# Ordering edges behind the two state copies of an RWKV-7 chain step

## The chip, the cores and the metric

One core of a Trainium2 chip runs the kernel. The metric is the device time of one launch in microseconds (us), lower is better. Before the change it is 1561.51 us, the median of three runs (1561.48 to 1563.06).

## What is computed

A decoder layer for one sequence of 1024 tokens and width 1024. One RMSNorm and one input projection feed two branches of 16 heads of 64 channels: RWKV-7 time mixing, which is a recurrence, and causal attention with three dilated windows. Each branch has a SiLU gate; the concatenated branches go through an output projection, a residual addition and a final RMSNorm. The change touches the recurrence alone:

```python
def step(state, inp):
    r_t, w_t, k_t, v_t, av_t, bv_t = inp
    sa = jnp.einsum('bhvk,bhk->bhv', state, av_t)
    state = (state * w_t[:, :, None, :] + sa[..., None] * bv_t[:, :, None, :]
             + v_t[..., None] * k_t[:, :, None, :])
    return state, jnp.einsum('bhvk,bhk->bhv', state, r_t)
```

## The kernel before

The program runs in three stages: the RWKV stage, with all projections of that branch woven in (the first 850 us), the attention stage with its own projections, and the output projection. Only the first is touched.

**Units and steps.** The 16 heads are taken as 8 pairs, and the 1024 tokens as two halves of 512, which gives 16 units. Inside a unit the recurrence is done in chunks of 64 tokens, 8 per unit, and each chunk in three steps of the `chain` (L636): `first` multiplies the state `Sd` into `z`, `second` multiplies `zd` with the inverted triangular matrix `U` into the other half of `z`, `third` multiplies `ud` into `T`. Each step is a TensorE (PE) matmul into PSUM followed by `spread` (L653), the **two copies** of the step: VectorE (DVE) copies one head's 64x64 block to SBUF (L656 or, with a scale, L659), ScalarE (ACT) the other's (L657, L660). The copies make `zd`, `ud` or the next `Sd`, which is the operand of the next step's matmul. So a unit is a serial chain of 24 steps: PE, then DVE and ACT, then PE again. Steps are counted here from 0, the first `z<-Sd` of a unit, to 23; copy n follows the matmul of step n, and step n+1 needs it.

**What is woven in.** `rwkv` (L297) has 24 slots (`NSLOT`) per unit, one for each chain step. Into each slot's list `ev[s]` go the chain step of unit p, and, at slots from the tables at the head of the file, the work on its neighbours: `finish` of unit p-1 (group norm and gate), `late` and `invert` of unit p+1 (transposes, and the inversion whose 15 column eliminations are two small DVE operations each, L570 into `TB` and L572 into `UB`, followed by a round trip through DRAM, L579 and L583, and four block steps of small matmuls m1 to m4, L590 to L634), `prepare` and `products` of unit p+2 (decays, products, masks, L394 to L554). After the list of a slot, `advance(n)` (L206) emits n = 4 matmuls (`pq`, L187) of the projections that later units and the attention stage need, with the loads, casts and subtractions of their weights (L176 to L179) and the work on their results (L221, L224, L257, L259).

**What sets the order.** Nothing of this is issued in the order written. The Tile framework schedules when the program is built: the priority of an instruction is its place in the program, and an engine is given the first ready instruction by priority. Where the head of the queue is not ready in its model, work from later slots is taken ahead. The order so found is fixed, and on the chip each engine runs its own list strictly in order, with semaphores between engines. The chain's steps come first in their slots:

```python
for s in range(NSLOT):
    for f in ev[s]:
        f()
    self.advance(n)
```

Of the kernel before, what the change touches and what calls it, by code (L numbers as in the profile page):

```python
# [12 lines left out]
AF = mybir.ActivationFunctionType  # L13
ALU = mybir.AluOpType
# [39 lines left out]
class Kern:  # L54
# [237 lines left out]
    def rwkv(self, pairs=range(NPAIR), apairs=range(NPAIR)):  # L292
        nc = self.nc
        with ExitStack() as ctx:
            P = lambda n, b=1, s=None: self.pool(n, b, s, ctx)
            self.ps_a = P("ps_a", 1, PSUM)
            self.ps_z = P("ps_z", 1, PSUM)  # L297
            self.ps_y = P("ps_y", 1, PSUM)
            self.ps_tr = P("ps_tr", 1, PSUM)
            self.mid = P("mid", 2)  # L300
            self.inv = P("inv", 1)
            self.pers = pers = P("pers")
            self.lng = P("lng", 3)
            self.dpool = P("dpool", 2, bass.MemoryType.DRAM)
            self.carry = pers.tile([128, 25], F32, name="carry")
            self.Us = [pers.tile([128, NC_ + 1, C], F32, name=f"U{i}") for i in range(2)]
            self.Vds = [pers.tile([128, NC_, 2, HD], F32, name=f"Vd{i}") for i in range(2)]
            self.Sds = [pers.tile([128, 2, HD], F32, name=f"Sd{i}") for i in range(2)]
            self.llo = [pers.tile([128, 128], F32R, name=f"llo{i}") for i in range(2)]
            self.zds, self.uds = ([pers.tile([128, 2, HD], F32, name=f"{nm}{i}") for i in range(2)] for nm in ("zd", "ud"))  # L310
            for u in self.Us + self.Vds + self.Sds + self.zds + self.uds:
                nc.gpsimd.memset(u, 0.0)
            for u in self.llo:
                nc.gpsimd.memset(u.bitcast(F32), 0.0)
            self.ARs = [pers.tile([128, NC_ * 192 + 2], F32, name=f"AR{i}") for i in range(3)]
            for a in self.ARs:
                nc.gpsimd.memset(a[:, NC_ * 192:], 0.0)
                a = self.c192(a)
                for e in range(2):
                    er = slice(e * 64, e * 64 + 64)  # L320
                    nc.gpsimd.tensor_copy(out=a[er, :, 0], in_=bc(self.ident[er, er].unsqueeze(1), (64, NC_, 64)))
            self.d0 = pers.tile([128, 2, C + 1], F32, name="d0")
            self.lw = pers.tile([128, NC_, C + 1], F32, name="lw")
            nc.gpsimd.memset(self.lw, 0.0)
            nc.gpsimd.memset(self.d0, 1.0)
            nc.gpsimd.memset(self.d0[:, :, C:C + 1], 0.0)
            bank = lambda p, tag: lambda: p.tile([128, 4, 128], F32, name="xq", tag=tag)
            ba = [bank(self.ps_a, "pa0"), bank(self.ps_a, "pa1")]
            tags = ("MV", "MV", "MV", "TU", "TU", "BK")
            for _ in self.prep_x(0, self.lng, tags, [bank(self.ps_proj, "proj")] * 2 + ba):  # L330
                pass
            units = [dict(h=h, pr=pr) for pr in pairs for h in range(2)]
            for i, d in enumerate(units):
                d["AR"], d["Vd"] = self.ARs[i % 3], self.Vds[i % 2]
            N = len(units)
            self.flow = self.stream(self.jobs(units, apairs))
            next(self.flow)
            self.taken = 1
            self.params(self.lng.tile([P_N, 128], F32, name="rows", tag="TU"),
                        self.ps_tr.tile([128, P_N], F32, name="prm_ps", tag="tr"))  # L340
            self.advance(6 * KT - 1)
            get = lambda n: units[n] if 0 <= n < N else None
            self.lora_w(units[0])
            for p in range(-2, N):
                dA, dI, dC, dF = get(p + 2), get(p + 1), get(p), get(p - 1)
                ev = [[] for _ in range(NSLOT)]
                put = lambda steps: [ev[s].append(f) for s, f in steps]
                if dC:
                    put(enumerate(self.chain(dC, get(p + 1) if dC["h"] == 0 else None)))
                if dF:  # L350
                    put(self.finish(dF))
                if dI:
                    put(self.late(dI))
                    put(self.invert(dI, self.Us[(p + 1) % 2]))
                if dA:
                    lag = WARM[p + 2] if p < 0 else 0
                    put([(n + lag, f) for n, f in self.prepare(dA) + self.products(dA)])
                if get(p + 3) and get(p + 3)["h"] == 0:
                    ev[12].append(lambda d=get(p + 3): self.lora_w(d))
                elif get(p + 3):  # L360
                    get(p + 3)["lw"] = get(p + 2)["lw"]
                if p == -2:
                    px = self.prep_x(1, self.lng, tags, ba)
                    for s in range(4):
                        ev[s].append(lambda: [next(px, None) for _ in range(2)])
                    ev[4].append(lambda: [None for _ in px])
                n = 5 if p < 0 else 2 if dA is not None and get(p + 3) is None else 4
                for s in range(NSLOT):
                    for f in ev[s]:
                        f()  # L370
                    self.advance(n)
            for _, f in self.finish(units[-1]):
                f()

# [261 lines left out]
    def chain(self, d, nxt):  # L636
# [3 lines left out]
        V, S, G = nc.vector, nc.scalar, nc.gpsimd  # L640
# [12 lines left out]
        def spread(out, q, scale):  # L653

            if scale is None:
                V.tensor_copy(out=out[er[0], 0], in_=q[0:64, 0:64])  # L656
                S.copy(out=out[er[1], 1], in_=q[0:64, 64:128])  # L657
            else:
                V.tensor_scalar(out=out[er[0], 0], in0=q[0:64, 0:64], scalar1=scale[0], scalar2=None, op0=ALU.mult)  # L659
                S.activation(out=out[er[1], 1], in_=q[0:64, 64:128], func=AF.Copy, scale=scale[1])  # L660

        def first(c):
            AR = d["AR"]
# [14 lines left out]
        def third(c):  # L678
            T = d["T", c // 4][:, c % 4]
            if c == 5:  # L680
                self.heads_out(d, 0)
            mm(T, f2(d["TU"][:, c])[:, 0:128], self.uds[c % 2], False, True)
            if c == NC_ - 1 and nxt is None:
                G.memset(self.Sds[0], 0.0)
                return
            dec, n = (nxt["dec"], 0) if c == NC_ - 1 else (d["dec"], c + 1)
            spread(self.Sds[(c + 1) % 2], T, [dec[:, e, n:n + 1] for e in range(2)])
            if n:
                values(n)
# [412 lines left out]
```

## Time and profile before

| | |
|---|---|
| median of three runs | 1561.51 us |
| the profiled execution's own time | 1562.53 us |
| its span, first to last instruction | 1560.8 us |
| PE busy | 1490.8 us, 96% |
| DVE busy | 1029.8 us, 66% |
| ACT busy | 891.8 us, 57% |
| GpSimd busy | 455.3 us, 29% |
| granted TensorE clock, mean | 0.997 |

The span leaves out 1.7 us around it. PE is busy nearly always, and what it waits is 70 us in all. A busy share over the whole span hides that the stages differ, so the profile is read stage by stage, and in the RWKV stage piece by piece within a unit, which repeats every 47.4 us. The instruction that waits on an engine is named with what released it; the releaser is inferred from semaphores.

### The profile page before, as it was taken

The numbers are of one execution on the slowest core, as the hardware profiler recorded it, in microseconds if no ns is written. First come the engines' busy times: TensorE is split into PE (matmuls) and PEld (weight loads), VectorE is DVE, ScalarE is ACT, GpSimd is POOL, SyncE is SP. The second block draws the span as 40 slices with busy tenths as digits, with TensorE's granted clock in tenths as the row PEclk, the third lists the DMA queues.
The fourth block names the chain that finished last, engine by engine and source line by source line (L and its number), as shares of the span: only waits on it lengthen the run. The fifth ranks groups of instructions, "written<-read, shape, count | busy, mean of one in ns | idle before, by whom it ended". The sixth has DMA issues, their size and how long they took to land.

```text
span 1560.8 us, 29095 instructions
## 1 busy us (share of the span) xinstructions
PE 1490.8 (96%) x10721; PEld 1211.8 (78%) x10721; DVE 1029.8 (66%) x2776; ACT 891.8 (57%) x2080; POOL 455.3 (29%) x563
## 2 busy tenths in 40 slices
PE   5999999999999999999999999999999999899997
PEld 4777777777777777777677788888888888787886
DVE  6867876777866768767644557666686676856144
ACT  6556666666666666665653556555565665645221
POOL 3122111121201212112111434333343344456442
PEclk9999999999999999999999999999999999999999
DMA  6221111111111111111111201111111111426452
GB/s 198 66 66 40 39 34 41 45 34 48 32 42 40 42 38 45 27 41 46 31 31 43 70 28 42 35 35 34 35 55 28 41 55 55 155 96 196 144 163 98
DMA packets 178829, 94.87 MB, mean 61 GB/s; under 512 B 58413, under 2 KB 164606, under 8 KB 178686
## 3 DMA queue, kind: packets, MB, share of 16 engines
q1 hardware_dynamic: 174942, 86.19, 19.4%
q10 hardware_dynamic: 3744, 6.82, 1.3%
q8 instruction: 84, 1.38, 0.4%
q14 instruction: 59, 0.48, 0.1%
HBM read 75.01 MB, written 17.83 MB: 59 GB/s over the span
## 4 chain that ended last, share of the span: by engine, by line
PE 67%; DVE 18%; ACT 10%; issue 3%; DMA 1%; POOL 1%; DVEq 0%; SPq 0%; POOLq 0%; ACTq 0%
PE pq L187 33%; PE oq L986 10%; PE T L645 4%; PE z L645 3%; PE o L932 3%; PE mp L859 2%; PE sp L892 2%; PE pa L529 2%; PE sp L912 1%; PE sp L911 1%; ACT zt L726 1%; DVE wl L179 1%; ACT MV L535 1%; PE x L621 1%; DVE I L424 1%
## 5 line engine op out<-in xcount | busy, mean ns | idle before, releaser
L187 PE MATMUL pq<-xh,wh 128*128 128x512 f32 x1040 | 428.9, 413 | 0.0
L187 PE MATMUL pq<-xl,wh 128*128 128x512 f32 x1040 | 416.4, 400 | 0.0
L187 PE MATMUL pq<-xh,wl 128*128 128x512 f32 x1040 | 294.8, 404 | 0.0
L187 PEld LDWEIGHTS pq<-xl,wh 128*128 128x128 f32 x1040 | 196.9, 189 | 32.0 <-DVE xl L166 0.2
L187 PEld LDWEIGHTS pq<-xh,wh 128*128 128x128 f32 x1040 | 196.5, 189 | 32.2 <-ACT xh L165 0.2
L187 PEld LDWEIGHTS pq<-xh,wl 128*128 128x128 f32 x1040 | 185.4, 189 | 31.9
L986 PE MATMUL oq<-ow,qr 128*128 128x512 f32 x512 | 161.9, 394 | 1.2 <-ACT ow L967 0.6
L920 POOL TENSOR_TENSOR pl<-p,ph 128x512 fp32r<-128x512 f32 (+2 forms) x96 | 102.2, 1071 | 202.5 <-ACT ph L919 182.3
L861 DVE CUSTOM_DVE_ANT_0 mp<-mp,maskq 128x512 f32<-128x512 f32 (+1 forms) x192 | 105.5, 570 | 67.6 <-PE mp L859 59.1
L915 ACT ACTIVATE p<-p 128x512 f32<-128x512 f32 (+2 forms) x144 | 64.6, 452 | 103.4 <-DVE p L914 102.5
L179 POOL TENSOR_TENSOR wl<-wraw,wh 128x512 fp32r<-128x512 f32 x64 | 85.2, 1351 | 110.5 <-ACT Sd L660 36.2
L981 POOL TENSOR_TENSOR vr<-kr,qr 128x512 fp32r<-128x512 f32 (+2 forms) x68 | 91.1, 1346 | 80.3 <-ACT qr L980 73.8
L986 PEld LDWEIGHTS oq<-ow,qr 128*128 128x128 f32 x512 | 95.9, 188 | 22.7 <-ACT ow L967 1.1
L986 PE MATMUL oq<-ow,vr 128*128 128x512 f32 x256 | 101.2, 395 | 2.0 <-POOL vr L981 2.0
L178 ACT CAST wh<-wraw 128x512 fp32r<-128x512 f32 x138 | 80.3, 618 | 39.2 <-PE pq L187 31.2
L980 ACT CAST qr<-kr 128x512 fp32r<-128x512 f32 (+2 forms) x68 | 40.1, 594 | 95.1 <-PE oq L986 49.8
L914 DVE TENSOR_TENSOR p<-sp,maskt 128x512 f32<-128x512 f32 (+2 forms) x144 | 65.2, 457 | 43.0 <-PE sp L912 41.5
L645 PEld LDWEIGHTS T<-ud,TU 128*128 128x128 f32 x256 | 40.8, 188 | 47.6 <-ACT ud L660 42.0
L660 ACT ACTIVATE Sd<-T,dec 64x64 f32<-64x64 f32 x120 | 36.9, 307 | 67.5 <-DVE Sd L659 66.2
L645 PE MATMUL T<-ud,TU 128*128 128x128 f32 x256 | 58.4, 310 | 16.8 <-ACT ud L660 15.6
L659 DVE TENSOR_SCALAR Sd<-T,dec 64x64 f32<-64x64 f32 x120 | 32.9, 274 | 60.4 <-PE T L645 58.2
L660 ACT ACTIVATE ud<-z,rn 64x64 f32<-64x64 f32 x128 | 39.3, 307 | 50.6 <-DVE ud L659 47.6
(236 smaller groups left out, 3173.5 us busy)
## 6 DMA issues: line engine op xcount, KB each, us to landing
wraw<-in_w_in_dram SPq DMA_DIRECT2D x138, 256.0 KB
kr<-mixd SPq DMA_DIRECT2D x60, 256.0 KB
oraw<-in_w_out_dram SPq DMA_DIRECT2D x16, 512.0 KB
xt<-in_x_dram SPq DMA_DIRECT2D x8, 512.0 KB
ld<-TU SPq DMA_DIRECT2D x32, 128.0 KB
mixd<-zt SPq DMA_DIRECT2D x16, 256.0 KB
mixd<-gt SPq DMA_DIRECT2D x16, 256.0 KB
xr<-in_x_dram ACTq DMA_DIRECT2D x16, 256.0 KB
```

Source lines behind the costliest of these rows:

```text
L178: nc.scalar.copy(out=wh[:, ks], in_=raw)
L179: eng.tensor_tensor(out=wl[:, ks], in0=raw, in1=wh[:, ks].bitcast(F32), op=ALU.subtract)
L187: return [lambda i=i, a=a, b=b: self.nc.tensor.matmul(q, lhsT=a, rhs=b, start=(i == 0), stop=(i == len(ops) - 1)) for i, (a, b) in enumera ...
L645: mm = lambda out, w, x, start, stop: nc.tensor.matmul(out, lhsT=w, rhs=f2(x), start=start, stop=stop, skip_group_check=True)
L660: S.activation(out=out[er[1], 1], in_=q[0:64, 64:128], func=AF.Copy, scale=scale[1])
L861: V.tensor_tensor_reduce(out=mp[:, :kn], in0=mp[:, :kn], in1=self.maskq[:, v0:v0 + kn], op0=ALU.add, op1=ALU.max, scale=1.0, scalar=-3e38, ...
L914: V.tensor_tensor(out=p[:, :qn], in0=sp[:, :qn], in1=self.maskt[:, u0:u0 + qn], op=ALU.add)
L915: S.activation(out=p[:, :qn], in_=p[:, :qn], func=AF.Exp)
L920: G.tensor_tensor(out=pl[:, :qn], in0=p[:, :qn], in1=ph[:, :qn].bitcast(F32), op=ALU.subtract)
L932: nc.tensor.matmul(oc, lhsT=v, rhs=w[:, :qn], start=(first and i == 0), stop=(last and i == len(prods) - 1), skip_group_check=True)
L981: nc.gpsimd.tensor_tensor(out=ml, in0=raw, in1=mh.bitcast(F32), op=ALU.subtract)
L986: nc.tensor.matmul(q, lhsT=m[:, i], rhs=v, start=(k == 0 and j == 0), stop=(k == 15 and j == 2))
```

## The change

`spread` keeps its two instructions in `self.copies`. In each slot that has a chain step, everything traced after that step in the same slot (the other work of `ev[s]` and that of `advance`) gets an ordering edge to the copy on its own engine: DVE work to the DVE copy, ACT work to the ACT copy. Such an edge has no semaphore; it fixes only that the engine's list has the copy first. Priorities stay as they were. Work on PE, GpSimd and the DMA queue of SyncE gets no edge. The second unit of a pair has no third copy in its last step; `self.copies` is empty there.

```diff
                 for s in range(NSLOT):
-                    for f in ev[s]:
-                        f()
-                    self.advance(n)
+                    with ExitStack() as order:
+                        for i, f in enumerate(ev[s]):
+                            f()
+                            if dC and i == 0:
+                                for ins in self.copies:
+                                    order.enter_context(self.tc.issue_after(ins.ins))
+                        self.advance(n)
...
             if scale is None:
-                V.tensor_copy(out=out[er[0], 0], in_=q[0:64, 0:64])
-                S.copy(out=out[er[1], 1], in_=q[0:64, 64:128])
+                a = V.tensor_copy(out=out[er[0], 0], in_=q[0:64, 0:64])
+                b = S.copy(out=out[er[1], 1], in_=q[0:64, 64:128])
             else:
-                V.tensor_scalar(out=out[er[0], 0], in0=q[0:64, 0:64], scalar1=scale[0], scalar2=None, op0=ALU.mult)
-                S.activation(out=out[er[1], 1], in_=q[0:64, 64:128], func=AF.Copy, scale=scale[1])
+                a = V.tensor_scalar(out=out[er[0], 0], in0=q[0:64, 0:64], scalar1=scale[0], scalar2=None, op0=ALU.mult)
+                b = S.activation(out=out[er[1], 1], in_=q[0:64, 64:128], func=AF.Copy, scale=scale[1])
+            self.copies = [a, b]
...
             if c == NC_ - 1 and nxt is None:
+                self.copies = []
                 G.memset(self.Sds[0], 0.0)
                 return
```

No instruction is added or taken away on any engine. The five lists are the same as before ahead of the chain (but for a few instructions at its start) and after it; what lies between is put in another order. Line numbers of the changed kernel are up to 6 higher (L656 is L660, L712 is L718).

**DVE, the end of a unit.** The list of VectorE from the copy of step 20 (`Sd`) to that of step 21 (`zd`) in one of the units, before:

```order
L659 TENSOR_SCALAR Sd_123<-T_5644,dec 64x64
L570 TENSOR_TENSOR TB<-UB,AB 64x15
L572 TENSOR_TENSOR UB<-UB,TB 64x15
L570 TENSOR_TENSOR TB<-UB,AB 64x28
L572 TENSOR_TENSOR UB<-UB,TB 64x2x14
L570 TENSOR_TENSOR TB<-UB,AB 64x39
L572 TENSOR_TENSOR UB<-UB,TB 64x3x13
L570 TENSOR_TENSOR TB<-UB,AB 64x48
L572 TENSOR_TENSOR UB<-UB,TB 64x4x12
L656 COPY zd_127<-z 64x64
```

And now, from the copy of step 19 to the first steps of the next unit:

```order
L663 TENSOR_SCALAR ud_128<-z,rn 64x64
L617 STREAM_TRANSPOSE UT<-U_118 128x512
L663 TENSOR_SCALAR Sd_123<-T_5644,dec 64x64
L660 COPY zd_127<-z 64x64
L663 TENSOR_SCALAR ud_129<-z,rn 64x64
L660 COPY zd_126<-z 64x64
L574 TENSOR_TENSOR TB<-UB,AB 64x15
L224 SCALAR_TENSOR_TENSOR ks_5920<-pq,om,shtmp 128x512
L576 TENSOR_TENSOR UB<-UB,TB 64x15
L179 TENSOR_TENSOR wl<-wraw,wh 128x512
```

The column operations (`TB`, `UB`) of the next unit's inversion stood ahead of their slots, between the copies of steps 20 to 23; now the first one stands behind copy 0 of the unit in whose slots it was written.

**DVE, the middle of the first half.** VectorE from the copy of step 5 (`Sd`) on, now; before, the column operations were over by step 4:

```order
L663 TENSOR_SCALAR Sd_122<-T_5339,dec 64x64
L718 TENSOR_REDUCE gs<-ysq 128x8
L574 TENSOR_TENSOR TB<-UB,AB 64x39
L67 TENSOR_SCALAR rs_x<-gs 128x8
L576 TENSOR_TENSOR UB<-UB,TB 64x13x3
L68 TENSOR_SCALAR rs_w<-rs_x 128x8
L419 TENSOR_SCALAR lw<-th 128x8x64
L70 TENSOR_SCALAR gr<-rs_w 128x8
L72 TENSOR_SCALAR rs_x<-rs_x 128x8
L574 TENSOR_TENSOR TB<-UB,AB 64x28
L77 TENSOR_TENSOR rs_w<-gr 128x8
L660 COPY zd_126<-z 64x64
```

The last column operations now run between those of the group norm's square root (`gs`, `rs_x`, `rs_w`, `gr`), and reach step 6.

**PE, steps 16 to 19.** TensorE from the matmul of step 17 (`T<-ud`) towards that of step 19 (`z<-zd`, which follows after two more `pq`), before:

```order
L645 MATMUL T_5644<-ud_129,TU 128x128
L645 MATMUL z<-Vd_121,MV 66x128
L187 MATMUL pq<-xh_78,wl 128x512 x4
L645 MATMUL z<-Sd_122,AR_143 66x128
L645 MATMUL T_5644<-Vd_121,MV 128x128
L645 MATMUL T_5644<-Sd_122,AR_143 128x128
L608 MATMUL dq<-Xs,UT 16x16 x32
L187 MATMUL pq<-xh_79,wh 128x512
L187 MATMUL pq<-xl_81,wh 128x512
```

And now:

```order
L649 MATMUL T_5644<-ud_129,TU 128x128
L649 MATMUL z<-Vd_121,MV 66x128
L187 MATMUL pq<-xl_81,wh 128x512
L612 MATMUL dq<-Xs,UT 16x16 x13
L649 MATMUL z<-Sd_122,AR_143 66x128
L649 MATMUL T_5644<-Vd_121,MV 128x128
L649 MATMUL T_5644<-Sd_122,AR_143 128x128
L612 MATMUL dq<-Xs,UT 16x16 x19
L187 MATMUL pq<-xh_79,wh 128x512
L187 MATMUL pq<-xl_81,wh 128x512
L649 MATMUL z<-zd_126,U_119 66x128
```

And now the list goes through to step 19: between two steps of the chain stood four projection matmuls, now one or two, and the block matmuls `dq` of the inversion, which stood behind step 18, lie on both sides of it.

## Rows read from the trace of the kernel before

**Rows 1.** The chain's stretch: its us; busy PE, PEld, DVE, ACT, POOL; clock; DMA.

```profile
118.50:850.20 731.70, 704.38 (x6731) 555.07 (x6729) 509.78 (x1615) 455.34 (x1202) 130.54 (x229) 1.00 0.15 39
```

**Rows 2.** What PE waited for there: total us, times, longest us.

```profile
PE T L645 <- ACT ud L660: 15.6, 28, 0.9
PE z L645 <- ACT zd L657: 4.9, 8, 1.5
```

**Rows 3.** As rows 1: steps 0-13, 14-23, the next unit's 0-13; 12 units' sum.

```profile
495.60:525.70 30.10, 28.69 (x176) 22.72 (x174) 26.38 (x71) 20.73 (x50) 8.05 (x12) 1.00 0.18 49
525.70:543.00 17.30, 17.30 (x273) 13.67 (x271) 8.65 (x38) 8.89 (x28) 1.18 (x5) 1.00 0.11 21
543.00:573.10 30.10, 28.21 (x172) 22.30 (x171) 25.77 (x72) 21.36 (x54) 6.50 (x11) 1.00 0.19 51
...
sum 568.50, PE 548.89 PEld 433.87 DVE 416.77 ACT 364.31 POOL 103.06; mean PE 22.87 PEld 18.08 DVE 17.37 ACT 15.18 POOL 4.29
```

**Rows 4.** The timeline from step 14 of one unit (start, us taken).

```profile
525.43 0.38 PE L645 MATMUL T<-ud,TU 128*128 128x128 f32 x2
...
525.85 0.28 DVE L659 TENSOR_SCALAR Sd<-T,dec 64x64 f32<-64x64 f32 x1 [0.50 <-PE T L645]
...
526.16 0.31 ACT L660 ACTIVATE Sd<-T,dec 64x64 f32<-64x64 f32 x1 [1.06 <-DVE Sd L659]
...
526.57 0.38 PE L645 MATMUL z<-Sd,AR 128*66 128x128 f32 x2
...
527.24 0.20 ACT L657 COPY zd<-z 64x64 f32<-64x64 f32 x1 [0.78 <-DVE zd L656]
527.47 0.40 PE L187 MATMUL pq<-xl,wh 128*128 128x512 f32 x1
...
528.17 0.38 PE L645 MATMUL z<-zd,U 128*66 128x128 f32 x2
...
528.48 0.69 PE L598 MATMUL xq<-U,LT 32*16 32x16 f32 x64
...
528.90 0.31 ACT L660 ACTIVATE ud<-z,rn 64x64 f32<-64x64 f32 x1 [1.45 <-DVE ud L659]
...
529.25 1.07 ACT L601 COPY Xs<-xq 16x128 f32<-16x128 f32 x4
```

**Rows 5.** A late copy in the same unit's first steps, and the inversion's DMAs.

```profile
502.76 0.47 SPq L579 DMA_DIRECT2D ud<-UB  x1
...
504.75 3.65 SPq L583 DMA_DIRECT2D U<-ud  x8
...
508.84 0.38 PE L645 MATMUL z<-zd,U 128*66 128x128 f32 x2
...
509.67 0.75 DVE L458 SCALAR_TENSOR_TENSOR AR<-ks,prm,W 128x512 f32<-128x512 f32 x1
...
510.33 0.27 DVE L659 TENSOR_SCALAR ud<-z,rn 64x64 f32<-64x64 f32 x1
...
511.07 0.31 ACT L660 ACTIVATE ud<-z,rn 64x64 f32<-64x64 f32 x1
...
511.43 0.49 PE L645 MATMUL T<-ud,TU 128*128 128x128 f32 x2 [0.62 <-ACT ud L660]
```

**Rows 6.** VectorE alone: column operations back to back, in the tail of that unit.

```profile
537.21 0.20 DVE L570 TENSOR_TENSOR TB<-UB,AB 64x48 f32<-64x48 f32 x1
537.45 0.20 DVE L572 TENSOR_TENSOR UB<-UB,TB 64x48 f32<-64x48 f32 x1
```

**Rows 7.** VectorE alone: column operations between others, in the next unit.

```profile
545.43 0.18 DVE L572 TENSOR_TENSOR UB<-UB,TB 64x39 f32<-64x39 f32 x1
545.54 0.17 DVE L708 TENSOR_SCALAR gs<-gs 128x8 f32<-128x8 f32 x1
545.64 0.18 DVE L570 TENSOR_TENSOR TB<-UB,AB 64x28 f32<-64x28 f32 x1
545.75 0.69 DVE L709 TENSOR_TENSOR Y<-Y,gs 128x512 f32<-128x512 f32 x1
```

## The prediction

> **What bounds the kernel now.** I read the busy table of the chain's stretch first, because the two order lists differ nowhere else. There PE is busy 704.4 of 731.7 us [rows 1]. All that an order can win is therefore the 27 us in which PE is idle; the rest of the span (PE's own work) stays. Second, what PE waits for in this stretch: `T<-ud` for the ACT copy of `ud`, 28 times and 15.6 us, `z<-zd` for that of `zd`, 8 times and 4.9 us [rows 2]. So the copies are indeed what ends most of PE's idle time, but they are late in 36 of 383 steps only. Third, where in a unit that is. I cut twelve units at step 14. In the first part, 30.1 us, PE is idle 1.4 us in one unit and 1.9 in the next, and DVE is busy 26.4 and 25.8 us, 88% and 86%. In the second, 17.3 us, PE has no idle time at all and DVE is busy for half of it [rows 3]. Over the twelve units PE idles 568.5 - 548.9 = 19.6 us, 1.64 us per unit, all of it in first parts.
>
> Fourth, a late copy. The `z<-zd` matmul starts at 508.84; DVE begins an operation of 0.75 us at 509.67 (L458, written in slot 8, ahead of copy 7), its copy of `ud` follows at 510.33, the ACT copy is over at 511.38, and PE, which has waited 0.62 us, goes on at 511.43 [rows 5]. An undisturbed step is faster. From `T<-ud` at 525.43 through the DVE copy, and the ACT copy that starts only when DVE's is over, to `z<-Sd` at 526.57 it takes 1.14 us. From there to the end of the ACT copy of `zd` it is 527.44 - 526.57 = 0.87 us, and from `z<-zd` at 528.17 to the end of that of `ud` 1.04 us [rows 4]. Three steps need 3.05 us, with PE's restart 3.1 us.
>
> **What the change moves.** The edges keep DVE and ACT from taking work of later slots ahead of a copy. I counted in the two order lists, as a mean over eleven full units, what stands in the first part (from step 0 to step 13) and what in the second.
>
> *DVE.* 25.5 of the 30 column operations (`TB`, `UB`) come over from the second part, where DVE was half idle, into the first. Also 1.5 weight subtractions (L179) and 0.5 shifts (L224) come over, while one L541 and one L593 leave; with 0.6 to 0.7 us each that is no change. The price of a column operation I bound from two rows. Back to back they start 0.24 us apart, because each needs the one before it [rows 6]. Standing between other work they start 0.10 to 0.11 us apart [rows 7]. So the first part's DVE work grows by 2.7 us at least (25.5 x 0.105) and by 6.1 us at most. In the new list about half stand alone, in steps 1, 2 and 4, and half between other work, the last ones among those of a square root; I take 4.4 us, and DVE's work in the first part becomes 26.1 (the mean of the two units) + 4.4 = 30.5 us.
>
> The Trainium skill has a rule that speaks against the change here: by VectorE: DVE Perf Modes, section The DRAIN you can't avoid, the next DVE operation cannot issue until the pipe of the one before has emptied. By it no column operation would be cheaper than its dependent spacing, and DVE's work would be the upper figure, 26.1 + 6.1 = 32.2 us. The trace does not agree: operations that take 0.17 to 0.18 us each start 0.10 us apart [rows 7].
>
> *PE.* Its own work is unchanged in sum, but it moves too: the first part has 67.2 instead of 57.5 projection matmuls, 0.23 us each (three start between 527.47 and 528.17), and the 32 `xq` matmuls, 0.69 us [rows 4]. That is 9.7 x 0.23 + 0.7 = 3.0 us more there (2.3 + 0.7), 28.5 + 3.0 = 31.5 us, and as much less in the second part, 14.3 us instead of 17.3 [rows 3]. The chain lags behind its cover in the first part and must catch up in the second, with less to cover it. Thirteen more changes between projection and chain matmuls in the whole chain I cost at nothing.
>
> *First part.* DVE's 30.5 us stand against PE's 31.5 + 1.64 = 33.1 us, 92% where it was 88% or less. Bounds: all of the 1.64 us of idle time goes (no copy is late any more, since nothing of a later slot stands ahead of it); or DVE can fill no larger share than now, 26.1/30.1 = 87%, and the part takes 30.5/0.867 = 35.2 us, 2.1 us more. I take 0.1 us more, close to the present. The late copy of rows 5 stood behind work of a later slot, which the edges forbid; but the column operations come in where it was. In the new list two scans, three column operations, four small operations of the square root and the 0.7 us gate operation (L259), all of slot 6 or earlier, stand between copies 6 and 7, about as much as before, and no edge moves them.
>
> *Second part.* Ten steps need 10.3 us of 14.3, so on the whole PE covers them. But steps 14 to 19 now have 15 projection matmuls where there were 22 and the `xq`. With these (3.5 us), the `dq` matmuls (0.7, taken as `xq`) and the chain's own (twelve, two records each 0.11 us apart, 2.6) PE has 6.8 us for six steps that need 6.2. Before it was 9.1. Into this margin fall four ACT copies of the inversion, 1.07 us [rows 4], behind the copy of step 16, and four like them behind that of step 18. A step whose ACT copy could start 1.82 us after the earlier step began (1.04 + 0.05 + 0.73) finds ACT taken to 2.1; 0.3 us late, twice per unit. Bounds: 0, if PE's lag absorbs it; 0.6 us, if neither does. I take 0.35.
>
> *DMAs and other queues.* The last column operation moves from step 4 to step 7, and the DRAM round trip of `U` with it. It takes from 502.76 to 508.40 to issue, and as the reads were released 2.0 us after the write was issued, I allow 2 us for their landing [rows 5]. `xq`, which needs it, stands in step 13, six steps of about 2 us later. So it is covered, by some 4 us; were that gone, `xq` would hold PE for the rest. SyncE's list keeps its order apart from the two small loads of L383 and L384. GpSimd's work follows its releasers, and PE's waits of rows 2 don't end with it: nothing.
>
> **The sum.** 0.1 + 0.35 = 0.45 us per unit, for the fourteen units that have all three kinds of neighbours: 6.3 us slower. The profiled execution's 1562.53 us would become 1568.8; it stands 1.0 us above the median of the runs, so the median becomes 1568. A measurement of this kernel can tell about 0.2%, 3 us.
>
> **Rivals.**
> 1. *The copies come in time.* Most waits of rows 2 end, and the second part's thin cover holds. For it: 20.5 of the 27 us end with these copies, and the operation of rows 5 goes from its place. Against it: DVE's load in the first part rises, and work of a copy's own or earlier slots stays ahead of it. Half to two thirds of 1.64 us per unit in fourteen units: 11 to 15 us faster, 1548. The point from which it decides: if fewer than about 12 `T<-ud` waits are left.
> 2. *Nothing to tell.* PE's own work sets 96% of the stretch, and late copies only change places: 1558.5 to 1564.5.
> 3. *DVE becomes the bound of the first part.* Column operations cost 0.24 us each wherever they stand, DVE's work is 32.2 us there, more than PE's 31.5; at the present 87% the part takes 37.1 instead of 33.1 us, 4 us per unit, 56 us and 1618; at 95% it is 33.9, 0.8 us, and with the second part's 0.35 16 us, 1578. Rows 7 speak against it, so it gets a small chance, with 1590 as a middle. The Trainium skill states it as a rule in the section named above (VectorE: DVE Perf Modes, The DRAIN you can't avoid).
>
> **How the numbers follow.** The forecast (a few to some 20 us slower) has 0.44, rival 1 0.30, rival 2 0.18, rival 3 0.08. Faster by over 0.2% is rival 1: 0.30. Within 0.2%: rival 2, 0.18. Slower by over 0.2%: 0.44 + 0.08 = 0.52. The range reaches up to 1585, the forecast's bounds (0.6 us in the second part, half of the 2.1 in the first, 1.65 x 14 = 23 us) and the lowest part of rival 3, and down to 1548, the middle of rival 1; what is left out is some 0.14 below and 0.06 above. The forecast's own part of it is 1565 to 1585.
>
> **What would show it.** In the changed kernel's profile, cut at step 14: first parts longer by about 3 us with PE's idle time 1.5 to 2.2 us and DVE over 90%; second parts 14 to 15 us long, with PE idle in steps 16 to 19, where there was none, released by the ACT copies of `Sd` and `ud`. The column operations should show starts 0.1 us apart between others. The attention stage must be as before. The prediction is wrong if PE's wait for `ud` falls below some 8 us in the stretch (rival 1), if second parts show no PE idle time, or if PE waits for `U` ahead of `xq`.

## The result, and the profile after

The changed kernel takes 1571.87 us, the median of four runs (1568.90 to 1574.14), against 1561.49 us before (1561.05 to 1563.06) on the same chip: a ratio of 1.0064, 95% interval 1.0045 to 1.0082. It is slower by 0.64%, 10.4 us. The profiled execution of the change is the lowest of its four, 1568.90 us; the mean granted clock was 0.999 in it and 0.994 to 0.995 in the other three. The two traces are therefore only 6.4 us apart: the chain's stretch is 8.3 us longer, and what lies behind it 1.7 us shorter (710.6 before, 708.9 now), with the same work and a granted clock of 1.00 instead of 0.99 there. So 8.3 of the 10.4 us stand in the traces; where the other three runs lose the rest no trace shows. All that follows is read from the chain's stretch, where the clock is 1.00 in both.

The windows of the stretch after the change, and of what follows it (columns as in [rows 1]):

```profile
118.30:858.30 740.00, 703.35 (x6731) 543.02 (x6728) 502.20 (x1616) 458.98 (x1205) 116.60 (x229) 1.00 0.15 38
858.30:1567.20 708.90, 689.88 (x3352) 579.32 (x3352) 434.44 (x971) 368.23 (x744) 295.52 (x264) 1.00 0.25 76
```

PE's busy time fell by 1.0 us (704.38 to 703.35) and its idle time rose from 27.3 to 36.7 us. The 8.3 us are 9.3 us more of PE's idle time less these 1.0 us, so it is idle time that decides, as the argument of the prediction has it. What PE waited for in the stretch after the change, the groups that answer to [rows 2] first:

```profile
PE T L649 <- ACT ud L664: 19.2, 30, 1.6
PE z L649 <- ACT zd L661: 9.7, 28, 0.4
PE z L649 <- ACT Sd L664: 2.2, 5, 1.0
PE dq L612 <- ACT Xs L605: 2.0, 13, 0.2
```

The waits for `ud` did not end, they grew from 15.6 to 19.2 us (30 instead of 28). The wait for `zd` comes 28 times instead of 8 and takes 9.7 us instead of 4.9. The wait for the state's own copy `Sd` came once before (0.4 us) and comes five times now, none of them in units 1 to 12. One group is new: `dq`, which waits for the inversion's copies `Xs`.

Where that is in a unit, by the windows. First one unit after the change, cut at step 14 as in [rows 3]:

```profile
500.70:534.10 33.40, 31.68 (x250) 24.36 (x248) 28.99 (x95) 23.21 (x55) 6.53 (x12) 1.00 0.13 34
534.10:548.40 14.30, 13.92 (x196) 10.85 (x196) 5.36 (x14) 6.96 (x23) 1.00 (x4) 1.00 0.21 48
```

Then the sums over the first parts of the twelve units 1 to 12, and over their second parts. Before:

```profile
sum 360.12, PE 340.51 PEld 268.87 DVE 312.87 ACT 252.70 POOL 86.09; mean PE 28.38 PEld 22.41 DVE 26.07 ACT 21.06 POOL 7.17
...
sum 208.44, PE 208.44 PEld 165.06 DVE 103.96 ACT 111.67 POOL 17.00; mean PE 17.37 PEld 13.76 DVE 8.66 ACT 9.31 POOL 1.42
```

After:

```profile
sum 398.89, PE 375.54 PEld 288.02 DVE 344.53 ACT 280.21 POOL 75.34; mean PE 31.29 PEld 24.00 DVE 28.71 ACT 23.35 POOL 6.28
...
sum 175.50, PE 172.29 PEld 135.22 DVE 62.62 ACT 85.88 POOL 15.12; mean PE 14.36 PEld 11.27 DVE 5.22 ACT 7.16 POOL 1.26
```

Each sum is of the windows' length, then busy time by engine. A first part grew from 30.01 to 33.24 us, and PE's idle time in it from (360.12 - 340.51) / 12 = 1.63 to (398.89 - 375.54) / 12 = 1.95 us. A second part shrank from 17.37 to 14.63 us, and PE, which had no idle time there, has 0.27 us. Together a unit has 0.58 us more of idle time and 0.09 us less of PE's busy time, 0.49 us, or 5.8 us over twelve units. Unit 0 took 2.0 us more (45.4 to 47.4), and the three units at the end 0.5 together; with the 5.8 that makes the 8.3.

The sums show something else. DVE's busy time in a first part went from 26.07 to 28.71 us, but its share stayed: 87% before, 86% now. ACT's went from 21.06 to 23.35 us. The prediction did not count what moves on ACT from one part to the other.

**Which queue a late copy stands in.** The timeline of the change around the longest wait that each of the units 1 to 12 has, 0.71 to 0.73 us at step 5's `T<-ud` (PE without the matmuls `pq` and `zq`, DVE with its half of the copy alone):

```profile
507.74 0.38 PE L649 MATMUL z<-zd,U 128*66 128x128 f32 x2
508.19 0.60 PE L502 MATMUL tq<-ident,BK 128*128 128x128 f32 x4
...
508.83 0.37 ACT L506 COPY TU<-tq 64x256 f32<-64x256 f32 x1 [2.10 <-PE tq L502]
509.41 0.20 ACT L457 COPY rn<-rn 64x8 f32<-64x8 f32 x1 [0.21 <-DVE rn L455]
509.45 0.27 DVE L663 TENSOR_SCALAR ud<-z,rn 64x64 f32<-64x64 f32 x1
509.62 0.37 ACT L507 COPY MV<-tq 64x256 f32<-64x256 f32 x1
510.00 0.36 ACT L506 COPY TU<-tq 64x256 f32<-64x256 f32 x1
510.38 0.37 ACT L507 COPY MV<-tq 64x256 f32<-64x256 f32 x1
510.77 0.31 ACT L664 ACTIVATE ud<-z,rn 64x64 f32<-64x64 f32 x1
...
511.13 0.49 PE L649 MATMUL T<-ud,TU 128*128 128x128 f32 x2 [0.71 <-ACT ud L664]
```

DVE's half of the copy is over at 509.72. ACT's half could follow, but ACT is in the middle of five copies, behind each other since 508.83, and starts it only at 510.77. The same place before the change:

```profile
501.63 0.60 PE L498 MATMUL tq<-ident,BK 128*128 128x128 f32 x4
503.00 0.38 PE L645 MATMUL z<-zd,U 128*66 128x128 f32 x2
...
502.64 0.20 ACT L453 COPY rn<-rn 64x8 f32<-64x8 f32 x1
502.75 0.36 ACT L502 COPY TU<-tq 64x256 f32<-64x256 f32 x1
...
503.88 0.37 ACT L503 COPY MV<-tq 64x256 f32<-64x256 f32 x1
504.49 0.31 ACT L660 ACTIVATE ud<-z,rn 64x64 f32<-64x64 f32 x1 [0.24 <-DVE ud L659]
504.85 0.49 PE L645 MATMUL T<-ud,TU 128*128 128x128 f32 x2 [0.54 <-ACT ud L660]
```

The same five copies stood between the same two state copies. But they began 0.36 us before `z<-zd`, and ACT was free again before DVE's half was over. PE waited here too, 0.54 us, in every second unit, but ACT itself had waited 0.24 us for DVE's half; now it is 0.72 us in all twelve units, with ACT busy. After the change the five copies begin 1.09 us after `z<-zd`. The work ahead of them is later. In PE's queue the transposes `tq` follow the transposes `sqt` of `sq` (L443). Before the change those ran from 498.74, ahead of step 3, from an `sq` that ACT had made in the unit before (486.93). Now ACT makes `sq` at 505.77, directly behind the copy of step 2 (505.44, 0.31 us), `sqt` follows at 506.55, in step 3, and `tq` in step 4.

ACT's half of a copy starts only after DVE's, so PE's wait ends with ACT's half whichever engine was late. What tells them apart is what ACT did ahead of its half. In the first parts of units 1 to 12 the timeline of the change has 43 such waits, and in all of them ACT went on to its half from other work without idle time. Before the change it was so in 18 of 28; in the other ten ACT had waited for DVE.

### The profile page after: what moved, and what is told of

Read it like the earlier page. It is cut to its first block, busy times and chain, and to the rows that moved or that the text cites. A ratio compares the mean times of both kernels' runs of the same rounds, so it can differ in the third digit from the quotient of the medians.

```text
span 1567.2 us, 29112 instructions
## 1 busy us (share of the span) xinstructions
PE 1488.2 (95%) x10721; PEld 1198.6 (76%) x10721; DVE 1021.0 (65%) x2776; ACT 894.1 (57%) x2080; POOL 439.1 (28%) x563
## 3 DMA queue, kind: packets, MB, share of 16 engines
q1 hardware_dynamic: 174942, 86.19, 19.2%
## 4 chain that ended last, share of the span: by engine, by line
PE 70%; ACT 14%; DVE 12%; issue 3%; DMA 1%; POOL 0%; DVEq 0%; SPq 0%; ACTq 0%; POOLq 0%
PE pq L187 33%; PE oq L992 10%; PE T L649 5%; PE z L649 4%; PE o L938 3%; PE mp L865 2%; PE pa L533 2%; PE sp L898 2%; ACT wh L178 1%; ACT zt L732 1%; DVE UB L576 1%; DVE TB L574 1%; PE sp L918 1%; ACT Vd L496 1%; ACT ud L664 1%
## 5 line engine op out<-in xcount | busy, mean ns | idle before, releaser
L187 PE MATMUL pq<-xh,wl 128*128 128x512 f32 x1040 | 298.4, 406 | 0.0
L660 DVE COPY zd<-z 64x64 f32<-64x64 f32 x128 | 27.5, 215 | 105.6 <-PE z L649 105.4
L178 ACT CAST wh<-wraw 128x512 fp32r<-128x512 f32 x138 | 80.0, 617 | 24.2 <-PE pq L187 15.7
L649 PE MATMUL T<-ud,TU 128*128 128x128 f32 x256 | 59.8, 315 | 21.0 <-ACT ud L664 19.2
L663 DVE TENSOR_SCALAR ud<-z,rn 64x64 f32<-64x64 f32 x128 | 34.9, 273 | 51.3 <-PE z L649 51.1
```

The source lines that it names most:

```text
L178: nc.scalar.copy(out=wh[:, ks], in_=raw)
L187: return [lambda i=i, a=a, b=b: self.nc.tensor.matmul(q, lhsT=a, rhs=b, start=(i == 0), stop=(i == len(ops) - 1)) for i, (a, b) in enumera ...
L649: mm = lambda out, w, x, start, stop: nc.tensor.matmul(out, lhsT=w, rhs=f2(x), start=start, stop=stop, skip_group_check=True)
```

## The experiments

Three theories, of which any mix could hold:
- **A, ScalarE's queue.** What the edges hold back on ACT is bunched behind one copy and delays ACT's half of the next.
- **B, VectorE's load.** The column operations that come into the first parts fill DVE, and the copies are late there. (This is what the prediction's first step rests on.)
- **C, cover.** Projection matmuls have moved into the first parts, and the second parts have too few to cover the chain's latency.

All times below are medians, and each ratio is to the kernel before on the same chip. The runs come from several chips, on which the kernel before has 1561.1 to 1562.0 us. In the table PE's idle time (us per unit) is worked out from the same two sums of windows over units 1 to 12 as above, and ACT and DVE are busy us per unit in first parts.

| kernel | time | ratio to before, interval | unit | idle, first | idle, second | PE busy | ACT | DVE |
|---|---|---|---|---|---|---|---|---|
| before | 1561.5 | | 47.38 | 1.63 | 0.00 | 45.75 | 21.1 | 26.1 |
| the change | 1571.9 | 1.0064, 1.0045-1.0082 | 47.87 | 1.95 | 0.27 | 45.65 | 23.4 | 28.7 |
| e1_dve_edge | 1569.0 | 1.0044, 1.0029-1.0059 | 47.78 | 1.23 | 0.56 | 45.99 | 21.4 | 28.0 |
| e2_act_edge | 1572.9 | 1.0076, 1.0059-1.0093 | 48.17 | 2.53 | 0.06 | 45.57 | 22.9 | 27.6 |
| e5_steps_0_13 | 1579.7 | 1.0116, 1.0101-1.0132 | 48.52 | 1.99 | 0.43 | 46.10 | 23.5 | 29.6 |
| e6_steps_14_23 | 1558.8 | 0.9984, 0.9975-0.9994 | 47.29 | 1.94 | 0.00 | 45.34 | 21.1 | 26.7 |
| e7_values_9 | 1570.2 | 1.0051, 1.0036-1.0067 | 48.01 | 2.02 | 0.27 | 45.71 | 23.2 | 28.6 |
| e8_rn1_late | 1566.0 | 1.0019, 1.0008-1.0030 | 47.40 | 1.52 | 0.27 | 45.62 | 23.4 | 28.6 |
| e9_cover | 1561.3 | 0.9996, 0.9987-1.0006 | 47.22 | 1.56 | 0.40 | 45.26 | 21.3 | 26.4 |
| e10_both_moves | 1566.2 | 1.0025, 1.0016-1.0035 | 47.63 | 1.61 | 0.27 | 45.74 | 23.2 | 28.6 |
| e11_rn1_cover | 1554.8 | 0.9952, 0.9939-0.9966 | 46.84 | 1.17 | 0.40 | 45.27 | 21.3 | 26.4 |
| e12_before_cover | 1566.7 | 1.0032, 1.0020-1.0044 | 47.80 | 1.80 | 0.23 | 45.77 | 20.4 | 24.7 |
| e14_late_edges_cover | 1566.5 | 1.0035, 1.0022-1.0048 | 47.74 | 1.54 | 0.27 | 45.93 | 19.0 | 24.5 |
| e15_dve_edge_cover | 1571.1 | 1.0058, 1.0045-1.0072 | 48.12 | 1.50 | 0.40 | 46.21 | 20.9 | 26.0 |

### One half of the edges at a time

**e1_dve_edge**: edges behind DVE's copy alone.

```diff
-            self.copies = [a, b]
+            self.copies = [a]
```

> Edges on VectorE alone (ScalarE is free to run ahead again). A unit took 47.4 us before and 47.8 with both edges. Theory A (ScalarE's queue: with its edge, the work of a slot stands bunched behind that slot's copy, and the next ScalarE copy waits behind it): the cost goes, 47.3 to 47.5 us per unit, 1560 to 1565 us, and the 0.7 us wait of T<-ud in step 5 is gone. Theory B (VectorE's load: all 30 column operations stand in steps 0 to 13 here too): 47.7 to 48.0 us per unit, 1567 to 1573 us. Theory C (cover: 65.5 projection matmuls stand in steps 0 to 13, 57.5 before, 67.2 with both edges): most of the cost stays, PE idle time of 0.1 to 0.4 us in steps 14 to 23 of each unit.

**e2_act_edge**: edges behind ACT's copy alone.

```diff
-            self.copies = [a, b]
+            self.copies = [b]
```

> Edges on ScalarE alone (VectorE runs ahead again; 10.5 of 30 column operations in steps 0 to 13, 64.0 projection matmuls there). Theory A: the cost stays, 47.7 to 48.0 us per unit, 1567 to 1573 us, and PE waits longest for ScalarE copies behind ScalarE work of the slot before. Theory B: the cost goes, 47.3 to 47.5 us, 1560 to 1565 us. Theory C: about half, 47.5 to 47.7 us.

With DVE's edges alone the kernel is 7.4 us slower than before, with ACT's alone 11.3 us. The second is the time that A gave. The first, 1569.0 us, is not: A had 1560 to 1565 and the wait at step 5 gone, but that wait is still there, 0.45 to 0.59 us in each of the units 1 to 12. The time alone would speak for B or C; the parts of the unit tell them apart. The sums of their first parts, e1_dve_edge and then e2_act_edge:

```profile
sum 383.11, PE 368.39 PEld 288.30 DVE 335.57 ACT 256.39 POOL 69.84; mean PE 30.70 PEld 24.02 DVE 27.96 ACT 21.37 POOL 5.82
```

```profile
sum 383.33, PE 352.92 PEld 279.09 DVE 331.69 ACT 274.24 POOL 64.96; mean PE 29.41 PEld 23.26 DVE 27.64 ACT 22.85 POOL 5.41
```

Both have some 28 us of DVE work in 31.9 us, a share of 88 and 87%. But PE idles 1.23 us in the first, less than before the change, and 2.53 us in the second. They differ in ACT: 21.4 against 22.9 us. One kind of instruction makes up most of that. The sums of L178 alone (ACT's casts of the projection weights) over the same first parts, of before and of e2_act_edge:

```profile
sum 360.12, ACT 14.31; mean ACT 1.19
```

```profile
sum 383.33, ACT 27.39; mean ACT 2.28
```

ACT's edges bring about two more of these casts per unit into the first part, as the whole change does (27.39 as well); DVE's edges do not (13.72 in e1_dve_edge). With DVE's edges alone the column operations are all in the first parts and PE idles less there than before, so B falls as the cause of the first parts' longer waits, and A is left. Of the 0.40 us per unit that e1_dve_edge takes more than before, 0.56 are idle time of the second parts and 0.24 are PE's busy time, less the 0.40 won in the first parts. The second parts' idle time is mostly one wait in each, of `z<-Sd` in step 15 (0.38 to 0.53 us). About as much of that wait, in step 9, is in the first parts:

```profile
PE z L649 <- ACT Sd L664: 13.1, 27, 0.7
```

Before the change it was 0.4 us, once.

### Edges in one part of a unit

**e5_steps_0_13**: edges in the first fourteen steps alone.

```diff
-                            if dC and i == 0:
+                            if dC and i == 0 and s < 14:
```

> Both edges, but only in steps 0 to 13 of a unit. The lists show 67.6 projection matmuls in these steps, as with all edges. Theory C: nothing is won, 47.7 to 48.0 us per unit, 1567 to 1573 us, with PE idle in steps 14 to 23 though no edge stands there. Theories A and B expect the same for steps 0 to 13 (PE idle 1.7 to 2.2 us per unit there, as with all edges) but, without C, no idle time in steps 14 to 23: 47.5 to 47.6 us, 1564 to 1567 us.

**e6_steps_14_23**: edges in the last ten steps alone.

```diff
-                            if dC and i == 0:
+                            if dC and i == 0 and s >= 14:
```

> Both edges, but only in steps 14 to 23. The lists show 57.0 projection matmuls in steps 0 to 13, as before the change, and 13.5 of 30 column operations there (4.5 before, 30 with all edges). Theory C: no idle time of PE in steps 14 to 23, though all the edges of these steps are there. Theory B, by the nine more column operations in steps 0 to 13: 0.1 us more per unit than before, 47.5 us, 1563 us. Theory A: as before, 47.4 us, 1561 us, or a little less, since copies 16 to 23 come no later. All expect 1559 to 1565 us; over 1567 none of the three holds.

The second parts' idle time belongs to the edges of the *first* steps: 0.43 us with no edge in the second part, none with edges there alone. That spoke for C. Two things none of the theories explains. Edges in steps 14 to 23 alone make the kernel a little faster than before (1558.8 us, 0.16%). A had allowed for a little, from copies that come no later, but PE's idle time rose and its busy time fell. And edges in steps 0 to 13 alone are worse than in all steps, by 7.8 us. Of the 0.65 us per unit that e5_steps_0_13 takes more than the change, 0.20 is idle time and 0.45 PE's busy time, with the same matmuls. What those records hold I can't read from the trace; this is open.

### Work taken out of ACT's way, edges kept

**e8_rn1_late**: in the five copies of the timeline above, `rn1` (L457) waits for DVE's `rn` (509.41, 0.21 us after the copy ahead), and the three copies behind it wait too. It is issued eight slots later (slot 10 instead of 2).

```diff
         def norm():
...
-            S.copy(out=d["rn1"], in_=rn[64:128])
...
         def bonus_parts():
...
+            S.copy(out=d["rn1"], in_=d["rn"][64:128])
```

> The changed kernel with one ACT copy of the norm (`rn1`, which waits for a VectorE operation and so holds ACT's queue) issued in step 10 instead of among the work ahead of step 4's copy; the edges stay. PE idles 0.72 us per unit at step 5's `T<-ud`, whose ACT copy stands behind `TU`, `rn1`, `MV`, `TU`, `MV`. Theory A: with `rn1` gone from there the wait shrinks by 0.3 to 0.5 us, and the time is 4 to 7 us under the changed kernel's (about 1565 to 1568). Theory B: VectorE's list is as before, the wait stays at 0.7 us, the time within 2 us. If the copy of `ud` is held by `TU` and `MV` alone, A falls in this form: then the wait stays as well, with ACT busy up to it.

1566.0 us, 5.9 us under the change. The timeline of its step 5:

```profile
506.34 0.38 PE L649 MATMUL z<-zd,U 128*66 128x128 f32 x2
...
507.43 0.36 ACT L506 COPY TU<-tq 64x256 f32<-64x256 f32 x1 [2.10 <-PE tq L502]
507.81 0.37 ACT L507 COPY MV<-tq 64x256 f32<-64x256 f32 x1
508.06 0.27 DVE L663 TENSOR_SCALAR ud<-z,rn 64x64 f32<-64x64 f32 x1
...
508.57 0.37 ACT L507 COPY MV<-tq 64x256 f32<-64x256 f32 x1
508.96 0.31 ACT L664 ACTIVATE ud<-z,rn 64x64 f32<-64x64 f32 x1
509.32 0.49 PE L649 MATMUL T<-ud,TU 128*128 128x128 f32 x2 [0.29 <-ACT ud L664]
```

The wait fell from 0.71 to 0.29 us, and in the stretch the waits of `T<-ud` from 19.2 to 13.1 us:

```profile
PE T L649 <- ACT ud L664: 13.1, 30, 1.6
```

The first parts' idle time fell by 0.43 us per unit, the second parts' stayed. DVE's work there is as before (28.6 us). That is A, by the place and the size that it gave; B expected no change by more than 2 us. ACT is still busy from 507.43 up to the copy of `ud`, so the 0.29 us that are left are those of `TU` and `MV`.

**e7_values_9**: the copies of `Vd` (L496), which stand ahead of step 12's copy, issued two slots earlier. **e10_both_moves**: that and `rn1` together.

```diff
-LATE = (0, 3, 11, 10)
+LATE = (0, 3, 9, 10)
```

> The changed kernel with the copies of the values (`Vd`, four ACT operations, 1.50 us) issued in step 9 instead of step 11; the edges stay. In the changed kernel's trace they stand on ACT just ahead of step 12's copy, and PE idles 0.39 us per unit at the next `z<-zd`. Theory A (work bunched behind one copy on ACT delays the next ACT copy): that wait goes, PE's idle time in the first parts falls from 1.93 to about 1.55 us per unit, and the time is some 5 us under the changed kernel's (about 1566 to 1567). Theory B (VectorE's load in the first parts sets the waits): DVE's work is the same, so the idle time stays within 0.1 us and the time within 2 us of the changed kernel's. Theory C (too few projection matmuls are left for the second parts) expects no change of the second parts' 0.27 us.

> Both moves on ACT at once, on the changed kernel: `Vd` in step 9 and `rn1` in step 10. Theory A: the two gains add up, PE's idle time in the first parts falls by 0.7 to 0.9 us per unit to 1.0 to 1.2, and the time is 9 to 12 us under the changed kernel's, at or under the kernel before (1560 to 1563). Theory B: no change by more than 2 us. If the first parts become shorter but the second parts' idle time grows by as much, it is theory C that decides: PE's work of its own then sets the unit and late copies only change places.

Both miss: 1570.2 us, within 2 us of the change, and 1566.2 us, no better than `rn1` alone. The waits of e7_values_9:

```profile
PE T L649 <- ACT ud L664: 18.9, 35, 1.6
PE bq L512 <- ACT Vd L496: 5.8, 14, 0.7
PE z L649 <- ACT zd L661: 4.5, 14, 0.4
```

The wait for `zd` went from 28 times and 9.7 us to 14 and 4.5, as A had it. A new one of the same size took its place: `bq`, whose PSUM tile has the same tag as the transposes that `Vd` is copied from, now follows directly and waits for these copies, 14 times and 5.8 us. In PE's queue it holds the chain as well as `zd` did. The numbers (1.7 us, idle time within 0.1 us) are those that B gave, but the waits moved as above, with DVE's work the same. A named the wait rightly and not what would be late next.

### Where the projection matmuls stand

**e9_cover**: the change, with the projection matmuls spread otherwise.

```diff
-                        self.advance(n)
+                        self.advance(n if n != 4 else 3 if s < 10 else 4 if s < 14 else 5)
```

> The changed kernel with the projection matmuls spread otherwise: three groups advanced per step in steps 0 to 9, four in steps 10 to 13, five in steps 14 to 23, instead of four everywhere. By the order list the first parts then have 60.0 projection matmuls per unit instead of 67.2 (57.5 before the change). Theory C: the second parts' idle time (0.27 us per unit) goes, and as first parts are not short of cover, the time falls by 3 to 4 us under the changed kernel's (about 1568). Theory A and B: the first parts' waits come at the same copies, with less beside them, so their idle time grows by a part of 7.2 x 0.23 = 1.7 us; at the most the time is 10 us over the changed kernel's.

1561.3 us, 10.6 us under the change and level with before. C's sign was right, but not its reason. The second parts, which got cover back, idle *more*, 0.40 instead of 0.27 us. The gain is 0.39 us of idle time in the first parts and 0.39 us of PE's busy time per unit, less the 0.13 us. The sums of its first parts, and of L178 alone in them:

```profile
sum 370.17, PE 351.47 PEld 274.23 DVE 316.79 ACT 255.49 POOL 66.01; mean PE 29.29 PEld 22.85 DVE 26.40 ACT 21.29 POOL 5.50
```

```profile
sum 370.17, ACT 13.68; mean ACT 1.14
```

With the matmuls, the two casts of weights per unit and 2.3 us of DVE's work have left the first parts: ACT's work there is back near what it was before the change. That fits A. By steps, the largest change is at step 13, whose wait falls from 0.38 us per unit to 0.03. In the change ACT's copy ahead of it stands behind the copies of `Vd` and an operation on projection results (L221 or L257), in e9_cover directly behind `Vd`. Step 5's wait stays at 0.71 us.

**e12_before_cover**, **e14_late_edges_cover** and **e15_dve_edge_cover** put the same line (the diff of e9_cover) into the kernel before, into e6_steps_14_23 and into e1_dve_edge.

> A control: the kernel before, with no edges, and the projection matmuls spread three, four and five groups per step. By the order list its first parts have 50.6 projection matmuls per unit instead of 57.5. Theory C (the edges make second parts short of cover, and this spread gives it back): the kernel before has no idle time in second parts that could be won, and loses cover in the first parts, so it comes out between no change and 7 us slower (1562 to 1569). Theory D (the spread is a better order of the matmuls by itself, edges or not): some 10 us faster, as on the changed kernel, about 1552.

> The kernel with edges in steps 14 to 23 alone (e6_steps_14_23, 1558.8 us), with the projection matmuls spread three, four and five groups per step; by the order list 51.8 instead of 57.0 stand in the first part. Its second parts had no PE idle time. Theory C: nothing to win there, 1558 to 1563. Theory D: some 10 us faster, about 1549.

> The kernel with the edges behind VectorE's copies alone (e1_dve_edge, 1569.0 us; PE idle 1.22 us per unit in first parts and 0.55 in second ones), with the projection matmuls spread three, four and five groups per step; 56.5 instead of 65.5 stand in the first part. Theory C: the 0.55 us of the second parts go (0 to 0.2 are left), 5 to 8 us: 1561 to 1564. Theory D: some 10 us or more, with the idle time of the second parts unchanged. If 0.55 us stay and the time as well, theory C falls.

None became faster: e12_before_cover is 5.6 us slower than before, where C had it, e14_late_edges_cover 7.8 us slower than e6_steps_14_23, and e15_dve_edge_cover 2.1 us slower than e1_dve_edge, where the intervals overlap. So the spread is no better order by itself, and theory D, which the expectations name so, falls. C falls with e15_dve_edge_cover: its second parts had 0.56 us to win, and 0.40 stayed, while the first parts' idle time rose from 1.23 to 1.50 us. e14_late_edges_cover lost more than C allowed, with idle time in second parts that had none. What the three have in common is that ACT's edges don't reach the first steps, and in the kernels that they start from no casts were pushed into first parts (1.19 us per unit before and in e6_steps_14_23, 1.14 in e1_dve_edge). In e12_before_cover and e15_dve_edge_cover the casts stay where they were. In e14_late_edges_cover they leave the first parts altogether:

```profile
sum 347.50, ACT 0.00; mean ACT 0.00
```

There the first parts' idle time falls by 0.41 us per unit, as in e9_cover (0.39), but 0.27 come back in the second parts and 0.59 in PE's busy time. So casts and idle time of the first parts go together in two kernels; that the casts are the cause is argued, not shown, as no run moved them alone. Why the spread costs PE's busy time in one kernel and saves it in the other is open.

**e11_rn1_cover**: e8_rn1_late and e9_cover together.

> The changed kernel with the copy `rn1` in step 10 (as in e8_rn1_late) and the projection matmuls spread three, four and five groups per step (as in e9_cover). Theory A: the two act at different places, so they add up. With `rn1` alone the kernel came 5.9 us under the changed one and with the cover alone 10.6 us under; together some 16 us: about 1555 to 1557, under the kernel before (1562). Were both the same microseconds of PE's idle time, it would be 1560 to 1561, as with the cover alone.

1554.8 us, the fastest of all, 0.48% under the kernel before (interval 0.34 to 0.61%). The two gains add up as expected (16.5 together is 17.1 here). Its stretch:

```profile
119.50:843.00 723.50, 696.71 (x6728) 545.88 (x6726) 492.92 (x1616) 457.22 (x1204) 109.38 (x229) 1.00 0.16 39
```

PE is idle for 26.8 us, against 27.3 before, and busy for 696.7, against 704.4. Waits of `T<-ud` (12.6 us) and `z<-zd` (8.2) are still there. So even this version does not win by ending the waits for the copies; its gain over before lies in PE's busy time.

## Why the prediction was right or wrong

**The time** came out as 1571.9, with 1568 forecast: the side was right, and the size roughly, 10.4 us for 6.3. The sum per unit was to be 0.45 us, and units 1 to 12 show 0.49. That they are so close is luck, since the terms are not those that I wrote.

**First part, +0.1 us of idle time: mis-sized, and for the wrong reason.** It is 0.31 us. The step that failed is "DVE's 30.5 us stand against PE's 31.5 + 1.64 = 33.1 us, 92%". DVE's work became 28.7 us and its share stayed at 86%, where over 90% was to show it. The 25.5 column operations came over, but DVE's work grew by 2.64 us only, near the lower bound of 2.7. I took 4.4 by letting half of them stand alone; some ten do around step 2 (503.9 to 506.4), but in steps 3 to 5 of the timeline most stand between other work. From the changed kernel, VectorE alone:

```profile
508.99 0.22 DVE L576 TENSOR_TENSOR UB<-UB,TB 64x63 f32<-64x63 f32 x1
509.13 0.19 DVE L455 RECIPROCAL rn<-rn 128x8 f32<-128x8 f32 x1
509.25 0.21 DVE L574 TENSOR_TENSOR TB<-UB,AB 64x60 f32<-64x60 f32 x1
```

Operations of 0.19 to 0.22 us start 0.12 to 0.14 us apart. So rival 3 fell. The rule that it rests on (the Trainium skill, VectorE: DVE Perf Modes, section The DRAIN you can't avoid) has the next operation wait until the pipe is empty, but the same section goes on that a next operation that is not held starts earlier, which the prediction left out. These rows, like [rows 7], show such earlier starts.

What I left out is the other engine that the edges bind. I counted moves on DVE and PE. On ACT 2.3 us per unit came into the first parts, and ACT's own queue holds the late copies: `ud` at step 5 (0.71 us), `zd` at step 13 (behind `Vd` and an operation on projection results), `ud` in the second part (below). e1_dve_edge and e2_act_edge put this down to ACT's edges in the main, and e8_rn1_late shows it for one copy.

**The operation of [rows 5] goes, and something else takes its place**: right in kind, but it is another engine's work at another place. In the unit of the window 500.7 to 534.1 the first part has one wait of `T<-ud` left, the 0.71 us shown at step 5, behind ACT's copies; every second unit, not this one, has one more at step 14, 0.66 to 0.69 us. And [rows 5] had been read for the wrong engine. DVE's half was over at 510.60, and ACT's began only at 511.07, because ACT had this ahead of it (the kernel before):

```profile
510.31 0.74 ACT L726 COPY zt<-yq 64x256 f32<-64x256 f32 x2
```

An undisturbed ACT half follows 0.03 us behind DVE's [rows 4], so 0.44 us of the 0.62 that I put down to DVE's operation were ACT's, already before the change.

**Second part, +0.35 us: 0.27, with the right place and half of the reason.** The timeline of the change:

```profile
537.91 0.53 ACT L605 COPY Xs<-xq 16x128 f32<-16x128 f32 x2
538.46 0.31 ACT L664 ACTIVATE Sd<-T,dec 64x64 f32<-64x64 f32 x1
538.48 0.36 PE L612 MATMUL dq<-Xs,UT 16*16 16x16 f32 x26 [0.15 <-ACT Xs L605]
...
540.17 1.06 ACT L616 COPY U<-dq 16x128 f32<-16x128 f32 x4 [0.43 <-PE dq L612]
540.50 0.28 DVE L663 TENSOR_SCALAR ud<-z,rn 64x64 f32<-64x64 f32 x1 [0.17 <-PE z L649]
541.26 0.31 ACT L664 ACTIVATE ud<-z,rn 64x64 f32<-64x64 f32 x1
541.62 0.49 PE L649 MATMUL T<-ud,TU 128*128 128x128 f32 x2 [0.23 <-ACT ud L664]
```

The second wait is the predicted one: four copies of 1.06 us behind the copy of one step, ACT's half of the next at 541.26, 0.23 us late. The first is not `z<-Sd` but `dq`, which waits for the copies `Xs` themselves. The other half of the reason, the thinner cover, did not hold: e9_cover gave the cover back and the idle time rose.

**PE's work, "unchanged in sum"**: nearly so here (0.09 us less per unit), but that is luck; see the last section. With it falls the first step, that an order can win only the 27 us of PE's idle time: e11_rn1_cover wins 7.7 us of its busy time and 0.5 of its idle time. The lengths of the parts, 33.1 + 0.1 and 14.3 + 0.35, came out as 33.24 and 14.63.

**The fourteen units alike**: only thirteen, 1 to 13, have all three kinds of neighbours, and unit 0, which has no unit before it, lost 2.0 us, 1.0 of it in idle time. The DMAs and SyncE, costed at nothing, did cost nothing: `xq` waits 0.2 us once in the stretch, for ACT.

**Rival 1** falls by its own point: 30 waits of `T<-ud` are left, not under 12. **Rival 2** falls with the interval, which begins at 0.45%. Yet edges in steps 14 to 23 alone would have fallen under it.

## What to carry to other kernels

An edge that holds other work behind an urgent instruction does not take that work away: it starts later and stands ahead of the next urgent instruction. So count what moves on *every* engine that the edges bind, and first on the one whose half of the copy comes last. Then look in each late copy's queue for the instruction that itself waits (here a small ACT copy behind a VectorE operation): moving that one out gave 6 us, while moving one that only stood there made the next PSUM user wait instead.

## What the runs showed of the hardware that was not expected

PE's busy time, as the profile counts it, is no constant of the program. With the same matmuls, their sum over twelve units goes from 543.2 us (e9_cover) to 554.6 us (e15_dve_edge_cover), 2%, by their order alone, while the granted clock of the stretch is 1.00 in both. The gain of e6_steps_14_23 over before is of that kind: 0.31 us more of idle time per unit and 0.40 us less of busy time. A reading that adds up PE's idle time alone misses half of such a change. The profile models the ends of matmuls, and its clock is rounded to two places, which could hide up to half a percent of the 2%; the units' lengths are not modelled, and they move with it. What the longer records wait for the trace does not name, and no run here isolates it.
